# Issuing a quarter of the selected branch's cache pages from GpSimd instead of the sync engine

## The chip, the core and the metric

The kernel runs on one core of one Trainium2 chip. The metric is the device time of one execution in microseconds; the time before is the median of three runs. The profile is of one execution of its own. The engines go by the profile's names: PE is TensorE (PEld its weight loads), DVE is VectorE, ACT is ScalarE, POOL is GpSimd, SP is the sync engine, which computes nothing and issues DMA transfers. A "q" behind an engine's name (SPq) means its instruction queue: register moves, semaphores and the issuing of transfers.

## The reference

One layer of a decoder for two groups at once: a prompt of 1024 tokens and 8 sample sequences of 4 new tokens each, with 8192 tokens of past. Mixer A is a gated MLP over chunks of 128; mixer B is sparse attention with three branches (compressed blocks, selected blocks, a sliding window). What matters here is the selected branch of the sample group, cut down:

```python
past = cache_kv[page_table]            # 8 sequences x 64 pages of 128 rows, slots k_cmp, v_cmp, k_sel, v_sel
imp = sum over grouped heads of p_cmp  # importance of each block of 64 rows, from the compressed branch
sel_idx = top_k(imp with forced first, current and previous blocks, 16)
p = masked_softmax(q . k_sel[sel_idx])
o_sel = p @ v_sel[sel_idx]
o = g0 * o_cmp + g1 * o_sel + g2 * o_win
```

The pages lie in a pool in DRAM; the table says which page a sequence's n-th one is, so every page's address is known only at run time.

## The kernel before

The kernel does not gather 16 blocks. For each of the 8 sequences it loads all 64 pages of the selected keys and values (tensor `psel`, one page is 128 partitions x 1 KB = 128 KB) and puts a mask of minus infinity on the blocks that were not chosen. The work is cut into 32 groups: group n is sequence b = n // 4 and part u = n % 4, with 16 pages, four for each c in 0..3. A group goes through three steps. `sel_scores(n)` takes a page buffer, loads the pages, multiplies on PE and ends in an exponent on ACT (lines L980, L982, L983: mask added and maximum on DVE, exponent on ACT). `sel_turn` transposes the probabilities on PE (L990) and copies them out on DVE (L991); for u = 0 POOL clears a small piece (L995) that DVE then fills (L996). `sel_values` multiplies them with the values and copies the result out on ACT (L1009); that copy is the last use of the buffer.

There are four page buffers (128 partitions x 16 KB each), used in turn by `page_buffer()`: a load waits until the values of the user four places before are done. The buffers are shared with three other users: `near_scores` (the window branch, twice), `ada_late` (eight 2 MB pieces of `w_ada`, L1052) and `ya_load` at the end (L1261, L1266).

Between the groups PE works at the prompt's attention: 32 units (query tile and head) in `step`, each with `scores` (L1127, L1134 on DVE, L1129, L1135 on ACT), `turn` (PE L1160, ACT and DVE L1164), `norm` and `values`. `norm` makes reciprocal sums on DVE (L1188, L1189) and spreads them on POOL into a tile of one buffer, tag f4 (L1191); `values` of the next step transposes that tile on PE (L1200), and ends with a sum on DVE (L1211, L1212) and one on POOL (L1213). The order of PE's work in this stage is written out by hand (a manual schedule): groups are spread over the units in proportion to the units' work by the list `due`. The order on every other engine is drawn up by the scheduler from modelled times and is fixed when the program is built; each engine runs its instructions in that order.

Pages are issued by `load_pages` in fours: one register load of four table entries from SBUF (L512), then for each page a little register arithmetic and the transfer (L522). The argument `share` says which of eight fours go to ACT's queue; for the selected pages it is empty, so all 512 go to SP. `issue_after` keeps a four's register load behind the third four before it on the same queue. `mm` (L56) is the helper behind most matrix products; a "t" in a row is any tile of the kernel.

Of the kernel before, what the change touches and what calls it, by code (L numbers as in the profile page):

```python
# [50 lines left out]
def step_kernel(tc, A):  # L51
    nc = tc.nc
    sync, act, dve, pool, pe = nc.sync, nc.scalar, nc.vector, nc.gpsimd, nc.tensor

    def mm(out, lhsT, rhs, start, stop):
        return pe.matmul(out, lhsT, rhs, start=start, stop=stop)  # L56
# [30 lines left out]
    def pM():  # L87
        return psum([128, 512], F32, "M", 4)
# [407 lines left out]
        return w1s[d // 8][:, (d % 8) * 128 + 64 * s:(d % 8) * 128 + 64 * s + 64]  # L496

    b1t = C2([128, 1])
    pages, starts, freed = ([], []), [], {}

    def load_pages(items, after=None, share=(1, 4, 6), depth=2):

        for n in range(0, len(items), 4):
            i = items[n][2]
            own = len(starts) % 8 in share
            queue, kind = (act, mybir.EngineType.Activation) if own else (sync, mybir.EngineType.SP)
            before = pages[own]

            def load():
                return nc.values_load_multi_w_load_instructions(  # L512
                    ptab[i // 64:i // 64 + 1, i % 64:i % 64 + 4], engines=[kind],
                    min_val=0, max_val=639, skip_runtime_bounds_check_because="the table was clamped on chip")[1]
            with ExitStack() as order:
                if len(before) >= depth:
                    order.enter_context(tc.issue_after(before[-depth].ins))
                if own and after is not None:
                    order.enter_context(tc.issue_after(after.ins))
                rs = load()  # L520
            for (dst, src, _), r in zip(items[n:n + 4], rs):
                d = queue.dma_start(dst, src[bass.ds(r, 1)].rearrange("g p c -> p (g c)"))  # L522
            before.append(d)
            starts.append(d)
# [5 lines left out]
    def compress_load(n):  # L530
        b, half = n // 2, n % 2
        home = "b" if n >= LATE and n % 2 else "a"
        st = (R2B if home == "b" else PG)([128, 32, 256], F32, "st", 1)
        load_pages([(st[:, i], A["pcmp"], b * 64 + half * 32 + i) for i in range(32)], freed.get(home),
                   () if n == 5 else (1, 4, 6))
        paged[n] = st, home
# [119 lines left out]
    for tt in range(9):  # L656
        n = 128 if tt < 8 else 32
# [6 lines left out]
    for tt in range(9):  # L664
        n = 128 if tt < 8 else 32
# [154 lines left out]
    n = 5  # L820
# [70 lines left out]
    def page_buffer():  # L891

        n = len(uses)
        uses.append(None)
        assert n < 4 or uses[n - 4] is not None
        return n, R3S([128, 4, 4, 256], F32, f"st{n % 4}", 1), uses[n - 4] if n >= 4 else None
# [63 lines left out]
    def sel_scores(n):  # L960
        b, u = n // 4, n % 4
        if u == 0:
            sel_state[b] = (R3([128, 4], F32, "nm4", 2), R3([128, 4], F32, "s4", 2), [])
        nm4, s4, outs = sel_state[b]
        qb = QB[:, b].rearrange("p h t g -> p (h t g)")
        use, st, after = page_buffer()
        load_pages([(st[:, c, k], A["psel"], b * 64 + 16 * c + 4 * u + k) for c in range(4) for k in range(4)],
                   after, (), 3)
        s = R3([128, 544], F32, "su", 2)
        w = 512  # L970
        if u == 0:
            w = 544
            pt = pM()
            for c in range(4):
                mm(pt[32 * c:32 * c + 32, 0:32], qb, k_new[:, 0], True, True)
            dve.tensor_tensor(s[:, 512:544], pt[:, 0:32], new_sel[:, b], op=OP.add)
        ps = pM()
        for c in reversed(range(4)):
            mm(ps[32 * c:32 * c + 32], qb, st[:, c, :, 0:128], True, True)
        dve.tensor_tensor(s[:, 0:512].rearrange("p (n i) -> p n i", i=64), ps.rearrange("p (n i) -> p n i", i=64),  # L980
                          MB[:, b, 8 * u:8 * u + 8, None].to_broadcast([128, 8, 64]), op=OP.add)
        dve.tensor_reduce(nm4[:, u:u + 1], s[:, 0:w], axis=AX.X, op=OP.max, negate=True)  # L982
        act.activation(s[:, 0:w], s[:, 0:w], AF.Exp, bias=nm4[:, u:u + 1], accum_out=s4[:, u:u + 1])  # L983
        return use, st, s
# [249 lines left out]
    def sel_step(m):  # L1234

        if m:
            while m - 1 not in turned:
                one_more()
            use, st, _ = held.pop(m - 1)
            sel_values(m - 1, use, st, turned.pop(m - 1))  # L1240
            if m % 4 == 0:
                later(sel_merge(m // 4 - 1), 2)
        if m < 32:
            held[m] = sel_scores(m)

            def turning():
                turned[m] = sel_turn(m, held[m][2])
                yield from ()

            later(turning(), 3)  # L1250
# [103 lines left out]
    for gr in range(2):  # L1354
        for j in range(4):
            for h in range(2):
                own = slice(64 * h, 64 * h + 64)
# [528 lines left out]
```

## Time and profile before

| what | value |
|---|---|
| time, median of three runs (lowest to highest) | 1950.87 us (1947.74 to 1951.81) |
| profiled execution, its own time | 1950.22 us |
| its span in the trace | 1948.2 us |
| granted TensorE clock, mean | 0.982 |
| DMA packets and bytes | 253606, 345.09 MB, mean 177 GB/s |
| selected pages issued by SP | 512 of 128 KB |
| stage of the selected branch, first to last page issue | 607 to 980 us |

A row of the busy table gives an engine's busy time, its share of the span and its count of instructions. A row of the chain gives shares of the span along the work that ended last, followed back from the end. A timeline row is start, length, engine, line, operation, output<-input and count, and in square brackets the idle time before it with what ended it. A row by source line gives counts with least, median and greatest duration in nanoseconds, and the first and last start. A row of waits gives who waited for what: microseconds in total, times, and (among waits of a stretch) the longest. A row of windows gives a stretch, its length, the busy time and count of PE, PEld, DVE, ACT and POOL, the granted clock, the DMA engines' share and GB/s.

### The profile page before, as it was taken

To read this page: it belongs to the slowest core of one execution; us is meant where nothing else is said; L and a number is where in the kernel's file an instruction comes from. 1 tells how busy PE (TensorE), PEld (TensorE's weight loads), DVE (VectorE), ACT (ScalarE), POOL (GpSimd) and SP (SyncE) were. 2 spreads that over 40 slices of the span, in tenths; PEclk is the share of its full clock that TensorE was granted. 3 is DMA by queue.
4 is the path that set the end of the run, shared out by engine and by line. 5 is a ranking of instruction groups with operands and counts; after the bars stand their busy time and mean duration, and the time that the engine had idled before them with its cause. 6 is when DMAs were issued, how large, how long until landed. Compare 5 with 4: busy or idle time off the path is not lost.

```text
span 1948.2 us, 43689 instructions
## 1 busy us (share of the span) xinstructions
PE 1844.1 (95%) x16037; PEld 1734.9 (89%) x16037; DVE 1177.1 (60%) x2549; ACT 790.5 (41%) x1606; POOL 468.6 (24%) x613
## 2 busy tenths in 40 slices
PE   5899999999999998989989999899999999999996
PEld 3799999999997776767779998899999999999996
DVE  6615311112107666666665678999999999757464
ACT  4313111112116554555641356434444344545342
POOL 2410100000001000000002411567777675201010
PEclk9899999999999998999999999999999999999998
DMA  9455657776648777777764454233322223857463
GB/s 331 138 170 157 203 165 234 233 224 198 210 153 262 246 222 233 226 233 225 239 237 154 140 164 154 72 105 106 110 90 73 77 85 97 286 185 229 135 193 91
DMA packets 253606, 345.09 MB, mean 177 GB/s; under 512 B 35248, under 2 KB 189264, under 8 KB 251216
## 3 DMA queue, kind: packets, MB, share of 16 engines
q1 hardware_dynamic: 205408, 261.86, 42.8%
q10 hardware_dynamic: 36896, 41.22, 6.7%
q0 software_dynamic: 11088, 39.21, 5.7%
q8 instruction: 127, 2.08, 0.4%
q14 instruction: 87, 0.71, 0.1%
HBM read 304.91 MB, written 41.43 MB: 178 GB/s over the span
## 4 chain that ended last, share of the span: by engine, by line
PE 78%; DVE 6%; DMA 4%; issue 4%; SPq 4%; ACT 3%; POOL 1%; DVEq 0%; ACTq 0%; POOLq 0%
PE t L56 75%; SPq L522 3%; PE t L1160 2%; DMA t<-w_ada 2%; DVE t L320 1%; DMA t<-t 1%; DMA t<-psel 1%; DVE t L1591 1%; PE t L990 1%; DVE t L1529 1%; DMA t<-xT 1%; DVE t L1530 1%; DVE t L1134 0%; ACT t L1135 0%; SPq L512 0%
## 5 line engine op out<-in xcount | busy, mean ns | idle before, releaser
L56 PE MATMUL t<-t,t 128*128 128x264 f32 (+12 forms) x15262 | 1766.4, 304 | 72.1 <-DVE t L173 14.8
L56 PEld LDWEIGHTS t<-t,t 128*128 128x128 f32 (+2 forms) x15102 | 1652.2, 169 | 123.1 <-issue 50.8
L320 DVE TENSOR_TENSOR t<-t,t 128x512 fp32r<-128x512 f32 (+2 forms) x478 | 389.1, 822 | 309.4 <-ACT t L319 289.4
L319 ACT CAST t<-t 128x512 fp32r<-128x512 f32 (+5 forms) x544 | 311.1, 589 | 413.0 <-PE t L56 313.5
L1591 DVE TENSOR_TENSOR t<-t,t 128x264 f32<-128x264 f32 (+2 forms) x366 | 106.9, 338 | 11.4 <-PE t L56 11.4
L1160 PEld LDWEIGHTS t<-t,t 128*128 128x128 f32 x528 | 58.0, 144 | 31.4 <-issue 14.5
L1528 ACT ACTIVATE t<-t,t 128x1072 f32<-128x1072 f32 x44 | 56.6, 1286 | 70.1 <-DVE t L1591 44.2
L1191 POOL COPY t<-t 128x256 f32<-128x256 f32 x32 | 13.0, 407 | 281.5 <-DVE t L1189 179.2
L1164 ACT COPY t<-t 128x512 f32<-128x512 f32 (+1 forms) x112 | 58.7, 569 | 47.7 <-PE t L1160 47.6
L683 ACT ACTIVATE t<-t 128x384 f32<-128x384 f32 (+1 forms) x48 | 22.2, 465 | 137.1 <-DMA t<-pcmp 68.5
L1529 DVE SCALAR_TENSOR_TENSOR t<-t,t,t 128x1072 f32<-128x1072 f32 x44 | 72.8, 1654 | 7.7 <-ACT t L1528 7.1
L1160 PE MATMUL t<-t,t 128*128 128x128 f32 x528 | 74.5, 280 | 0.7 <-DVE t L1212 0.3
L1135 ACT ACTIVATE t<-t,t 128x640 f32<-128x640 f32 (+3 forms) x64 | 56.1, 877 | 41.3 <-DVE t L1134 36.4
L1720 POOL TENSOR_TENSOR t<-t,t 128x384 f32<-128x384 f32 (+1 forms) x12 | 13.9, 1190 | 225.9 <-ACT t L1787 225.9
L1134 DVE TENSOR_REDUCE t<-t 128x1 f32<-128x640 f32 (+3 forms) x64 | 58.8, 920 | 15.0 <-PE t L56 13.6
L685 POOL DMA_DIRECT2D t<-t x16 | 8.5, 533 | 241.6 <-DVE t L684 186.8
L1530 DVE SCALAR_TENSOR_TENSOR t<-t,t,t 128x1072 f32<-128x1072 f32 x44 | 65.1, 1479 | 0.0
L1554 POOL TENSOR_TENSOR t<-t,t 128x512 f32<-128x512 f32 x21 | 35.9, 1708 | 103.9 <-DMA t<-w_up 66.5
L1622 POOL TENSOR_TENSOR t<-t,t 128x1024 f32<-128x1024 f32 x22 | 54.3, 2468 | 16.3 <-ACT t L1621 16.3
L980 DVE TENSOR_TENSOR t<-t,t 128x512 f32<-128x512 f32 x32 | 22.1, 690 | 44.1 <-PE t L56 44.0
L1409 POOL TENSOR_TENSOR t<-t,t 128x384 f32<-128x384 f32 (+1 forms) x24 | 28.0, 1168 | 67.6 <-DVE t L1408 64.5
L320 DVE TENSOR_TENSOR t<-t 128x384 fp32r<-128x384 f32 (+1 forms) x66 | 36.1, 572 | 12.9 <-ACT t L319 12.9
(286 smaller groups left out, 1279.1 us busy)
## 6 DMA issues: line engine op xcount, KB each, us to landing
t<-psel SPq DMA_DIRECT2D x512, 128.0 KB
t<-pcmp SPq DMA_DIRECT2D x332, 128.0 KB
t<-w_down SPq DMA_DIRECT2D x120, 256.0 KB
t<-t POOLq DMA_DIRECT2D x50, 528.0 KB, 4.5
t<-w_up SPq DMA_DIRECT2D x96, 256.0 KB
t<-pcmp ACTq DMA_DIRECT2D x180, 128.0 KB
t<-w_ada SPq DMA_DIRECT2D x16, 1024.0 KB
t<-w_t ACTq DMA_DIRECT2D x52, 256.0 KB
```

What stands on the lines that cost most here:

```text
L56: return pe.matmul(out, lhsT, rhs, start=start, stop=stop)
L319: act.copy(hi, t)
L320: dve.tensor_tensor(lo, t, hi.bitcast(F32), op=OP.subtract)
L522: d = queue.dma_start(dst, src[bass.ds(r, 1)].rearrange("g p c -> p (g c)"))
L1134: dve.tensor_reduce(m4[:, branch, h:h + 1], ps[:, :, 0:w], axis=AX.XY, op=OP.max, negate=True)
L1135: act.activation(P[:, 0:L].rearrange("p (a c) -> p a c", a=2), ps[:, :, 0:w], AF.Exp, bias=m4[:, branch, h:h + 1], accum_out=s4[:, branch, ...
L1160: pe.transpose(pt[:, c:c + 128], probs[branch, h][:, 128 * b:128 * b + 128], ident)
L1164: (act.copy if w > 2 else dve.tensor_copy)(probs[branch, h][:, 128 * k:128 * (k + w)], pt[:, c:c + 128 * w])
L1528: act.activation(acc[:, 0:w], up[:, 0:w], AF.Identity, scale=cw[:, n, 0:1], bias=cw[:, n, 3:4])
L1529: dve.scalar_tensor_tensor(acc[:, 0:w], up[:, 1:1 + w], cw[:, n, 1:2], acc[:, 0:w], op0=OP.mult, op1=OP.add)
L1530: dve.scalar_tensor_tensor(acc[:, 0:w], up[:, 2:2 + w], cw[:, n, 2:3], acc[:, 0:w], op0=OP.mult, op1=OP.add)
L1591: dve.tensor_tensor(o, by4(banks[c][:, c0:c0 + n], n), other(c, c0, n) if other else o, op=OP.add)
```

## The change

Of a group's four fours the last (n = 12, which is c = 3) is issued by GpSimd; the first three stay on SP. The new value "pool" of `share` picks it, and GpSimd gets a list of its own for `issue_after`, so its register load stays behind the third four before it on GpSimd's queue. The compressed pages keep their rule. From this place on every line number is one higher in the changed kernel.

```diff
-    pages, starts, freed = ([], []), [], {}
+    pages, starts, freed = ([], [], []), [], {}
...
-            own = len(starts) % 8 in share
-            queue, kind = (act, mybir.EngineType.Activation) if own else (sync, mybir.EngineType.SP)
+            own = 2 if share == "pool" and n == 12 else int(len(starts) % 8 in share) if share != "pool" else 0
+            queue, kind = ((sync, mybir.EngineType.SP), (act, mybir.EngineType.Activation),
+                           (pool, mybir.EngineType.Pool))[own]
             before = pages[own]
...
         load_pages([(st[:, c, k], A["psel"], b * 64 + 16 * c + 4 * u + k) for c in range(4) for k in range(4)],
-                   after, (), 3)
+                   after, "pool", 3)
```

## The prediction

> **What bounds the kernel now.** I read the page first: its busy shares and the chain that ended last.
>
> ```profile
> span 1948.2 us, 43689 instructions
> PE 1844.1 (95%) x16037; PEld 1734.9 (89%) x16037; DVE 1177.1 (60%) x2549; ACT 790.5 (41%) x1606; POOL 468.6 (24%) x613
> PE 78%; DVE 6%; DMA 4%; issue 4%; SPq 4%; ACT 3%; POOL 1%; DVEq 0%; ACTq 0%; POOLq 0%
> ```
>
> TensorE bounds the whole, but 4% of the chain (some 78 us) stands on SP's queue, an engine that computes nothing. The change touches only the selected branch's pages, so the second view is the timeline of SP around them.
>
> ```profile
> 607.29 43.37 SPq L522 DMA_DIRECT2D t<-psel  x64
> ...
> 832.05 77.20 SPq L522 DMA_DIRECT2D t<-psel  x112
> ...
> 969.83 10.59 SPq L522 DMA_DIRECT2D t<-psel  x16
> 980.52 0.38 SPq L1261 DMA_DIRECT2D t<-t  x1
> 980.99 0.42 SPq L1266 DMA_DIRECT2D t<-w_ba  x1
> ```
>
> From 607.29 to 980.42 SP issues 512 pages, 16 for each of 32 groups, with no long hole: 373.1 us, or 11.66 us a group. In the long undisturbed run a page takes 77.20 / 112 = 0.69 us. Next the same stretch by kinds of instruction, count and nanoseconds (least/median/most), then a zoomed piece of the chain.
>
> ```profile
> L522 SPq FUSED_REGOPS  x512: 37/37/43, 607.1 to 980.0; - x171
> L522 SPq MOVE t<-psel x512: 29/29/38, 607.2 to 980.0; - x171
> L522 SPq DMA_DIRECT2D t<-psel x512: 332/333/1757, 607.3 to 980.1; - x171
> L512 SPq TENSOR_LOAD <-t x128: 295/301/315, 606.7 to 978.0; - x128
> ```
>
> ```profile
> 901.21 0.30 SPq L512
> 903.62 0.30 SPq L512
> ...
> 908.92 3.01 DMA t<-psel
> ...
> 912.06 1.29 PE t L56 x8
> ```
>
> One register load and four page transfers repeat every 903.62 - 901.21 = 2.41 us, 0.60 us a page: 333 + 37 + 29 ns of instructions, a quarter of the 301 ns load, and gaps of issue. The rest up to 0.69 is occasional long transfers (the 1757 ns maximum). The chain runs along these issues, through one landing of 3.01 us, into TensorE. TensorE takes groups at this pace, and between 600 and 1000 us it waited for these (microseconds in total, times, longest); below them the instruction that follows every group's scores, and what SP's queue waited for:
>
> ```profile
> PE t L990 <- ACT t L983: 12.0, 13, 2.5
> PE t L56 <- DMA t<-psel: 10.2, 4, 4.1
> ```
>
> ```profile
> L980 DVE TENSOR_TENSOR t<-t,t x32: 681/691/692, 627.5 to 985.8; 128x512 f32<-128x512 f32 x32
> ```
>
> ```profile
> SPq L522 <- DMA t<-w_ada: 19.1, 11, 3.1
> SPq L522 <- PE t L56: 4.0, 7, 1.5
> SPq L522 <- ACT t L1078: 1.2, 1, 1.2
> ```
>
> L980 follows each group's scores: (985.8 - 627.5) / 31 = 11.56 us a group, almost SP's 11.66. So the two are balanced, SP just the slower, and the price of that is 10.2 us of TensorE in four waits. That is the whole prize that the profile shows. SP itself hardly ever waits for a buffer (4.0 + 1.2 us): the buffers are free before SP gets to them. The 19.1 us behind w_ada are transfers that land late, and stay.
>
> **The change, part by part.** The sum is made against the profiled execution, 1950.22 us (1948.2 of span, 2.0 around it), 0.65 us under the median 1950.87.
>
> *Removed from SP.* For each group the last quarter goes: 1 TENSOR_LOAD and 4 pages, 2.41 us; over 32 groups 77 us at the undisturbed spacing, 128 x 0.69 = 88 us at the real one. SP keeps 12 x 0.69 = 8.3 us a group, plus its share of everything else it did in the 373.1 us (373.1 - 512 x 0.69 = 20 us, 0.6 a group): 8.9 against TensorE's 11.2 (11.56 less 10.2 / 31). SP then runs ahead until it meets the buffers' release, which is what is late next: four buffers, so about three paces or 30 us of lead where no other load sits between. I take it that the page waits go.
>
> *What the four waits are worth.* The largest is the last one, with ScalarE idle beside it:
>
> ```profile
> 984.23 1.50 PE L56 MATMUL t<-t,t 128*32 128x512 f32 x8 [4.05 <-DMA t<-psel]
> 986.87 0.59 ACT L1164 COPY t<-t 128x512 f32<-128x512 f32 x1 [6.36 <-PE t L1160]
> ```
>
> Nothing else holds TensorE there, so I count 4.05 in full. Its follow-up loads (L1261, at 980.52, waiting behind the last 16 pages on SP) come earlier too; w_ba at 980.99 does not lose. The other three make 10.2 - 4.05 = 6.15 us. Behind them stand waits for the exponent (L990 on L983, 12.0 us in 13) that could grow when TensorE is denser; I count four fifths, 4.9 us. Gain: 4.05 + 4.9 = 9 us.
>
> *Added to POOL.* Each group brings POOL one register load and four transfers with a runtime address, into its in-order stream between L1191 (the normalisers' spread), L1213 (an output sum) and L995 (a memset). POOL has never done this form; the nearest rows are its stores of the same 128 KB shape (L476), its slowest small stores (L741), and ScalarE's queue for the load.
>
> ```profile
> L476 POOL DMA_DIRECT2D o_rows<-t x18: 519/542/776, 52.6 to 113.8; - x18
> DMA to landing us min/median/max: 2.0/4.1/6.2
> ```
>
> ```profile
> L741 POOL DMA_DIRECT2D o_wsk<-t x8: 540/540/912, 589.7 to 598.9; - x8
> ```
>
> ```profile
> L512 ACTq TENSOR_LOAD <-t x45: 304/310/509, 75.9 to 558.1; - x45
> ```
>
> ```profile
> L1191 POOL COPY t<-t 128x256 f32<-128x256 f32 x32 | 13.0, 407 | 281.5 <-DVE t L1189 179.2 <-PE t L1200 39.2 <-ACT t L1202 13.8
> ```
>
> ```profile
> L1200 PE MATMUL t<-t,t x64: 272/273/422, 620.5 to 998.6; 128*128 128x128 f32 x64
> ...
> its engine sat idle before it (us, times) until:
>   POOL t L1191: 0.5, 2
> ```
>
> Low end: 4 x 0.542 + 0.310 + 4 x (0.037 + 0.029) = 2.75 us a group, 88 us in all. High end: 4 x 0.912 + 0.509 + 0.264 = 4.4 us, 141 us in all. I take the low one, since L476 has the shape. What covers it: POOL idled 281.5 us before L1191 alone, and only 2 of 32 L1200 transposes waited for L1191, 0.5 us together. Were that cover gone in every group, 32 x 2.75 = 88 us would be exposed; I charge 1 us for the two places that have no slack. A landing of 4.1 us (2.0 to 6.2) instead of SP's 3.01 costs nothing while the pages are issued a pace or more ahead.
>
> *Added wait.* POOL's first page of a group waits for the buffer, that is for the values of four groups before (L1009). Behind it in the queue stand L1191, L995 and L1213; TensorE's L1200 waits for the first, VectorE for the other two. SP had 5.2 us of such waits because it ran late; POOL has as many as the program's order gives it: bounded by 0 and, if one per group stood for a whole pace, by 32 x 11.2 = 358 us. I take 0, since the release and L1191 both follow TensorE's fixed order.
>
> *Traffic.* The bytes stay. The transfer engines have room:
>
> ```profile
> 850.00:900.00 50.00, 46.49 (x514) 34.83 (x510) 33.28 (x81) 29.87 (x68) 2.63 (x7) 0.95 0.67 198
> 604.00:1000.00 396.00, 359.14 (x4213) 275.50 (x4214) 259.03 (x696) 226.50 (x600) 29.34 (x72) 0.97 0.74 230
> ```
>
> The last three columns are granted clock, DMA share and GB/s. Pages alone move 198 GB/s at a share of 0.67, so full engines would give some 296 GB/s (an estimate from that row): 16 pages, 2.10 MB, in 7.1 us, well under 11.2. Issue is the limit, not the engines. [...]
>
> Sum: -9 + 1 = -8; 1950.2 - 8 = 1942.
>
> **The rivals.**
>
> *No change: another wait takes the place (about 1949, 1947 to 1953).* For it: 12.0 us already go to the exponent, and the clock was 0.95 in one of the stretches above; if a denser TensorE lost 0.02 of clock over 396 us, 8 us would be gone. [...] Against it: ScalarE is busy 226.50 of 396, VectorE 259.03, and the largest wait had nothing behind it.
>
> *Slower: POOL's queue holds the normalisers (about 1967).* A block of 2.75 us, or a wait for a buffer, stands ahead of L1191 in the queue, L1200 comes late, and TensorE, whose order is fixed, stops. If ten groups lose a block each: 1950.2 - 10.2 + 10 x 2.75 = 1967. It decides from 10.2 / 2.75, about four, exposed groups on. For it: the program's order on POOL is drawn up from modelled times, and the f4 tile has one buffer. Against it: the 281.5 us of idleness and 0.5 us of waits above. [...]
>
> *The pages were not the limit.* TensorE would then wait for psel as before with SP idle. The 11.56 beside 11.66 speaks against it; time 1950, inside the first rival.
>
> **How the numbers follow.** Forecast (page waits go, POOL stays covered) 0.66, its own range 1936 to 1946; no change 0.17; POOL's queue 0.17. Low end of the range: 1935, the 10.2 us plus half as much again from the 12.0 us of exponent waits moving, which I can't exclude. High end: to reach 8 in 10 it takes in the no-change case and the first exposed groups, 1950.2 - 10.2 + 5 x 2.75 = 1954. A measurement of this kernel tells 0.2%, 3.9 us, from no change; so faster 0.66, same 0.17, slower 0.17.
>
> **What would show it.** Right: SP's timeline in runs of 12 pages with waits on buffers (for TensorE or L1010 ScalarE copies) in place of unbroken issue; TensorE's waits for psel under 2 us; four POOL page transfers of about 0.54 us a group; the pace of L981 near 11.2 us; L1201 waiting for L1192 under 2 us. Wrong: POOL transfers well over 1 us, L1201 waiting for L1192 by 10 us or more, or the psel waits gone and the exponent's waits up by as much.

## The result and the profile after

The changed kernel takes 1933.87 us (median of 6, 1926.5 to 1937.59) beside 1949.93 us for the kernel before (median of 6) on the same chip: ratio 0.9919, 95% interval 0.9904 to 0.9935. It is faster, by 16 us or 0.8%, where the prediction had 8 us, and 1.1 us below the low end of its range. The profiled execution took 1933.99 us.

The order of the instructions on TensorE, VectorE and ScalarE is the same in both kernels (all 2549 rows of VectorE and 1606 of ScalarE match one by one; of TensorE's 16037, ten narrow matmuls change places with one close by); only GpSimd's and SP's differ. So the two traces can be laid side by side matmul by matmul. Line numbers after are one higher. First the page of the changed kernel: span, busy times, chain.

```profile
span 1932.4 us, 43957 instructions
PE 1842.7 (95%) x16037; PEld 1735.2 (90%) x16037; DVE 1173.3 (61%) x2549; ACT 789.2 (41%) x1606; POOL 540.8 (28%) x741
```

TensorE is as busy as before (1842.7 to 1844.1): no work went, only idle time. GpSimd gained 72 us. Next the chain of waits from 600 to 1000 us by line, before and after:

```profile
by line: PE t L56 40.7%; SPq L522 14.2%; PE t L1160 8.8%; issue 6.7%; DMA t<-psel 2.9%; PE t L990 2.7%; DVE t L1134 2.2%; ACT t L1135 2.2%; SPq L512 2.1%; DMA t<-w_ada 1.8%; ACT t L1164 1.8%; ACT t L983 1.5%; DMA t<-t 1.5%; ACT t L1129 1.2%
```

```profile
by line: PE t L56 57.7%; PE t L1161 11.7%; PE t L991 4.1%; DVE t L1135 3.1%; ACT t L1165 2.5%; ACT t L1136 2.5%; issue 2.4%; ACT t L984 2.3%; PE t L1201 1.7%; DVE t L865 1.5%; DVE t L992 1.3%; DVE t L1128 1.0%; DVE t L1165 1.0%; ACT t L1130
```

SP's page issue held 14.2% of this stretch and its register loads 2.1%; in the second line, which lists shares down to 1.0%, neither appears. Now everything of the pages (rows: count, least/median/most ns; who waited for them: us, times; landing), and SP's timeline in the second half of the stage, after:

```profile
L523 POOL DMA_DIRECT2D t<-psel x128: 546/546/628, 603.9 to 956.5; - x128
...
who waited for it (us, times):
  POOL t L523: 17.6, 8
  PEld t L56: 0.5, 2
...
DMA to landing us min/median/max: 2.6/4.1/6.7
```

```profile
821.86 0.82 SPq L1053 DMA_DIRECT2D t<-w_ada  x2
826.53 64.05 SPq L523 DMA_DIRECT2D t<-psel  x84
891.45 0.81 SPq L1053 DMA_DIRECT2D t<-w_ada  x2
897.84 17.28 SPq L523 DMA_DIRECT2D t<-psel  x24
...
954.67 7.50 SPq L523 DMA_DIRECT2D t<-psel  x12
964.56 0.38 SPq L1262 DMA_DIRECT2D t<-t  x1
```

No matmul waits for a page any more (before: 10.2 us in four waits); two weight loads do, 0.5 us together (before: two, 3.1 us). SP's queue now has holes, 821.86 + 0.82 to 826.53 for one. The waits between 600 and 1000 us say for what (us in total, times, longest), on SP, GpSimd and TensorE:

```profile
SPq L523 <- PE t L56: 62.6, 17, 6.0
...
SPq L1053 <- PE t L56: 13.9, 5, 8.2
```

```profile
POOL t L523 <- PE t L56: 25.0, 12, 6.2
...
POOL t L523 <- DMA t<-psel: 17.6, 8, 4.4
```

```profile
PE t L991 <- ACT t L984: 12.1, 14, 2.5
```

SP waits 62.6 us for buffers that TensorE still reads: it runs ahead, as forecast. GpSimd waits too, 25.0 us for buffers and 17.6 us behind its own earlier transfers, and nobody pays for it. The wait for the exponent is what it was (12.0 us in 13).

**Where the 15.7 us of the profiled spans went** (1948.15 - 1932.41). Both traces have 16037 matmuls; I cut them at the 5100th and the 9550th, which enclose the selected stage.

| stretch | before, us | after, us | difference |
|---|---|---|---|
| start to matmul 5100 | 591.34 | 591.51 | +0.2 |
| matmul 5100 to 9550 | 412.08 | 399.31 | -12.8 |
| of it TensorE idle | 38.26 | 26.41 | -11.9 |
| matmul 9550 to the last | 930.88 | 932.43 | +1.5 |
| last matmul to the last issue of o_y | 4.64 | 4.64 | 0 |
| last issue of o_y to the end | 9.21 | 4.52 | -4.7 |

The last row has nothing to do with pages at first sight. It is read from the instructions of the kernel's closing line, where each engine's queue ends with instructions that the profile calls DRAIN (of GpSimd's three the first is the long one; least/median/most in ns, first and last start in us), before and after:

```profile
L1871 POOLq EVENT_SEMAPHORE  x4: 17/17/17, 1947.4 to 1948.0; - x4
L1871 POOLq DRAIN  x3: 40/107/12252, 1935.1 to 1947.9; - x3
L1871 SPq DRAIN  x3: 7/7/7, 1942.2 to 1947.6; - x3
```

```profile
L1872 POOLq DRAIN  x3: 40/113/4255, 1924.0 to 1932.1; - x3
L1872 SPq DRAIN  x3: 7/7/7, 1931.5 to 1931.9; - x3
```

Before, GpSimd's DRAIN runs from 1935.1 for 12.25 us and ends at 1947.35; GpSimd's first semaphore instruction of that line follows at 1947.4, 5 us after SP's first DRAIN (1942.2). After, it lasts 4.26 us and ends at 1928.3, 3.2 us before SP's first (1931.5), so here SP's is the later one. In all 13 profiles below the program ends 0.8 to 0.9 us (once 1.0) after the later of the two, the end of GpSimd's long DRAIN or of SP's first.

There is a second effect inside the stage. Rows of windows on TensorE: stretch, length, busy time and count, granted clock, DMA share, GB/s, in the kernel before, right after the wait of 4.05 us at 984:

```profile
985.17:988.58 3.41, 3.41 (x16) 0.50 1.02 391
```

Half clock for 3.41 us. What it costs is seen from the same 16 matmuls on TensorE's timeline, before and after:

```profile
984.23 1.50 PE L56 MATMUL t<-t,t 128*32 128x512 f32 x8 [4.05 <-DMA t<-psel]
985.66 1.97 PE L1160 MATMUL t<-t,t 128*128 128x128 f32 x8
987.28 2.17 PE L56 MATMUL t<-t,t 128*128 128x512 f32 x8
```

```profile
974.43 1.09 PE L1161 MATMUL t<-t,t 128*128 128x128 f32 x8
975.28 1.56 PE L56 MATMUL t<-t,t 128*128 128x512 f32 x8
```

From the first start to the last end these 16 take 985.66 to 989.45, 3.79 us, against 974.43 to 976.84, 2.41 us: 1.38 us more, for the 2.92 us of half clock that fall on them (985.66 to 988.58). That is 0.47 us for each, or 1.6 us for a segment of 3.41. So in the kernel before some of TensorE's waits cost their length and this on top: of the four waits for pages, the 4.05 us had this segment behind it, the one of 2.66 us that ends at 755 shares 10.2 us of half clock with a wait for the exponent right after it, and the other two (2.23 and 1.26 us) had none.

### The profile page after: what moved, and what is told of

Its sections match the earlier page's. It is cut to its first block, busy times and chain, and to the rows that moved or that the text cites. A ratio compares the mean times of both kernels' runs of the same rounds, so it can differ in the third digit from the quotient of the medians.

```text
span 1932.4 us, 43957 instructions
## 1 busy us (share of the span) xinstructions
PE 1842.7 (95%) x16037; PEld 1735.2 (90%) x16037; DVE 1173.3 (61%) x2549; ACT 789.2 (41%) x1606; POOL 540.8 (28%) x741
## 2 busy tenths in 40 slices
DMA packets 241320, 345.10 MB, mean 179 GB/s; under 512 B 35248, under 2 KB 172880, under 8 KB 238928
## 4 chain that ended last, share of the span: by engine, by line
PE 83%; DVE 8%; ACT 4%; issue 2%; DMA 1%; POOL 1%; SPq 0%; DVEq 0%; ACTq 0%; POOLq 0%
PE t L56 79%; PE t L1161 2%; DVE t L320 1%; DMA t<-t 1%; PE t L991 1%; ACT t L319 1%; DVE t L1135 1%; DVE t L1531 1%; DVE t L1592 1%; DVE t L1530 1%; ACT t L1165 1%; ACT t L1136 1%; ACT t L984 0%; DVE t L338 0%; POOL t L1623 0%
## 5 line engine op out<-in xcount | busy, mean ns | idle before, releaser
L523 POOL DMA_DIRECT2D t<-psel x128 | 70.4, 550 | 63.8 <-PE t L56 25.0
L1165 ACT COPY t<-t 128x512 f32<-128x512 f32 (+1 forms) x112 | 58.5, 568 | 38.6 <-PE t L1161 38.4
L1136 ACT ACTIVATE t<-t,t 128x640 f32<-128x640 f32 (+3 forms) x64 | 56.1, 877 | 35.6 <-DVE t L1135 31.0
L1192 POOL COPY t<-t 128x256 f32<-128x256 f32 x32 | 13.1, 411 | 166.0 <-DVE t L1190 112.9
L711 POOL TENSOR_TENSOR t<-t,t 128x512 f32<-128x512 f32 (+1 forms) x12 | 12.3, 1041 | 125.4 <-DVE t L702 97.4
```

Source lines behind the costliest of these rows:

```text
L1136: act.activation(P[:, 0:L].rearrange("p (a c) -> p a c", a=2), ps[:, :, 0:w], AF.Exp, bias=m4[:, branch, h:h + 1], accum_out=s4[:, branch, ...
L1165: (act.copy if w > 2 else dve.tensor_copy)(probs[branch, h][:, 128 * k:128 * (k + w)], pt[:, c:c + 128 * w])
```

## The experiments

All ratios are to the kernel before, run on the same chip beside the experiment, with 95% intervals; waits for psel are those of matmuls. "Stage" is matmul 5100 to 9550, "end" the last row of the table above. The columns behind the ratio are of the profiled executions:

| kernel | ratio | waits for psel, us (times) | stage, us | half clock in it, us | GpSimd's transfers | its DRAIN, us | end, us |
|---|---|---|---|---|---|---|---|
| before | 1 | 10.2 (4) | 412.1 | 20.5 | 127 | 12.25 | 9.2 |
| quarter (the change) | 0.9919 [0.9904, 0.9935] | 0 | 399.3 | 17.1 | 255 | 4.26 | 4.5 |
| quarter again | 0.9899 [0.9878, 0.9921] | 0 | 398.0 | 13.7 | 255 | 4.25 | 4.5 |
| eighth, odd groups | 0.9888 [0.9874, 0.9902] | 0 | 396.3 | 10.2 | 191 | 8.18 | 5.1 |
| eighth, even groups | 0.9913 [0.9898, 0.9927] | 0 | 397.2 | 13.7 | 191 | 8.18 | 5.1 |
| half | 0.9932 [0.9919, 0.9945] | 0 | 405.0 | 17.1 | 383 | 6.54 | 3.6 |
| all on GpSimd | 1.0218 [1.0199, 1.0238] | 28.1 (8) | 455.8 | 58.0 | 639 | 10.14 | 7.1 |
| quarter on ScalarE's queue | 1.0062 [1.0049, 1.0075] | 0 | 418.3 | 27.3 | 127 | 12.25 | 9.2 |
| pages on SP, work on GpSimd | 0.9995 [0.9984, 1.0007] | 6.5 (3) | 411.6 | 20.5 | 127 | 12.25 | 9.2 |
| quarter, last 4 groups only | 0.9949 [0.9929, 0.9969] | 6.1 (2) | 406.3 | 20.5 | 143 | 3.76 | 3.6 |
| quarter, first 16 groups only | 0.9938 [0.9916, 0.9959] | 3.4 (2) | 404.9 | 20.5 | 191 | 8.17 | 5.3 |
| 128 small transfers on GpSimd | 0.9983 [0.9970, 0.9995] | 9.2 (3) | 411.9 | 20.5 | 255 | 4.25 | 4.1 |
| 16 small transfers on GpSimd | 0.9967 [0.9954, 0.9981] | 6.4 (3) | 406.4 | 17.1 | 143 | 3.76 | 4.3 |

The theory after the result was: SP's issue is what TensorE waited for, any relief of SP takes the waits away, and the half clock behind each wait goes with it. The rivals: GpSimd's extra work changes something by itself (the clock, the program's end); the gain needs a certain queue or a certain share; and, once the end had shown itself, that the end is a matter of the number of GpSimd's transfers or of something else.

**Half as much moved (odd groups).**

```diff
-                   after, "pool", 3)
+                   after, "pool" if u % 2 else (), 3)
```

> The last four pages go to GpSimd only in odd groups, an eighth of all pages. Theory (SP's issue pace held TensorE): SP keeps 14 pages a group, 14 x 0.69 + 0.6 = 10.3 us against TensorE's 11.2, so it is already fast enough: waits of TensorE for psel fall from 10.2 us to under 3, and TensorE's last product comes 8 to 12 us earlier than before (1934.3 in the trace of before, 1923.3 in that of the change). Rival (the gain goes with the share moved): half of it, about 5 us of psel waits left and the last product near 1929. On top of either, 4.7 us of the change's gain lie after the last product; theory: they hang on where the engines' instruction streams end and not on the pages, so they may come or not here, time 1935 or 1940; rival (they come from GpSimd being at work): about 1937.

Measured 0.9888, 1925.7 us. Sixty-four pages off SP's queue are enough: no matmul waits for a page any more. The last product came at 1913.3, 21 us earlier than before and 10 earlier than with the change, more than either side expected. That it looks faster than the quarter is mostly clock: its profiled execution had 10.2 us of half clock in the stage and 10.9 behind it, where the quarter had 17.1 and 18.7; 14.7 us less at 0.47 is 6.9 us. The repeat of the quarter below has an interval that overlaps with this one.

**Twice as much moved.**

```diff
-            own = 2 if share == "pool" and n == 12 else ...
+            own = 2 if share == "pool" and n >= 8 else ...
```

> Two fours of a group's four go to GpSimd, 8 pages, some 5.6 us a group. Theory: SP at 6 us a group and GpSimd at 5.6 plus 1 us of its own work are both far under 11.2; psel waits under 2 us, the last product within 2 us of the change's 1923.3, time within 4 us of 1934. Rival (GpSimd's in-order queue holds the normalisers): L1201 waits for L1192 by 5 us or more, time 1940 to 1960.

Measured 0.9932: no more gain than with the quarter. The waits for pages are gone there too, yet the stage is 5.7 us longer than the quarter's: 4.4 us more in which TensorE counts as busy and 1.2 us more idle, with the same 17.1 us of half clock. The scheduler also drew up another order on VectorE and ScalarE for this kernel (65 of 2549 and 43 of 1606 rows stand in another place than in the change); whether the larger share or the order makes the difference was not separated.

**The same quarter on ScalarE's queue.**

```diff
-            own = len(starts) % 8 in share
+            own = 1 if share == "act" and n == 12 else int(len(starts) % 8 in share) if share != "act" else 0
...
-                   after, (), 3)
+                   after, "act", 3)
```

> The same quarter goes to ScalarE's queue in place of GpSimd's. Theory (only SP's relief counts): psel waits under 2 us as with the change; but ScalarE issues some 2 us a group in its in-order stream, and its results are on the path, so TensorE's waits for ScalarE (L984, L1136, L1010; 12.1 + 3.7 + 0.4 us with the change) grow by 2 to 15 us; time 1936 to 1950. [...]

Slower, 1.0062, although SP is relieved just as much and no wait for a page is left; the 1959.2 us lie above the 1936 to 1950 expected. ScalarE's computing stands behind its page issues, and TensorE behind that; one wait of the stage before, then those in this kernel:

```profile
PE t L56 <- ACT t L1135: 3.7, 9, 0.7
```

```profile
PE t L991 <- ACT t L984: 16.7, 16, 3.8
PE t L56 <- ACT t L1136: 10.0, 9, 3.5
...
ACT t L1165 <- DMA t<-psel: 11.1, 8, 2.1
...
ACT t L984 <- DMA t<-psel: 7.6, 2, 4.4
```

The exponent's wait grew from 12.0 to 16.7 us and L1136's from 3.7 to 10.0; L1165 and L984 are ScalarE's own work, held up behind a page that waited for an earlier one (11.1 + 7.6 us). This is the slow rival of the prediction, on another queue, where it is real: the same pages cost or gain by what stands behind them. A part may belong to the order: some 50 rows each of VectorE and ScalarE stand in another place in this kernel than in the change, and that was not separated.

**The pages on SP, extra work on GpSimd.**

```diff
+        for _ in range(22):
+            pool.memset(R3([128, 32], F32, "pad", 1), 0.0)
```

> All pages stay on SP; GpSimd gets 22 small memsets a group, about 2.7 us, as much as the issuing takes it. Theory (GpSimd has room, SP's pace holds): psel waits stay near 10 us, L1201 waits for L1192 under 2 us, the last product within 2 us of before's 1934.3; the end after it is 9.4 us from the last output's issue as before or 4.6 as with the change, and if it is 4.6 the end hangs on GpSimd's instruction stream: time 1950 or 1945. Rival (GpSimd's time is on the path): L1201 waits for L1192 by 5 us or more, time 1955 or more.

0.9995, no difference. The waits for pages were 6.5 us and not near 10, and the last product of the profiled execution, one of the two slowest of twelve, came 4.4 us later than before's, where 2 were expected. GpSimd being busier by itself gains nothing, neither in the stage nor at the end, where the DRAIN stays at 12251 ns with 694 more GpSimd instructions in the program than before.

**The change again, beside the next three.**

> The changed kernel itself once more, beside the next three, on whatever chip they get. First measured at 0.9919 [0.9904, 0.9935] of before. If that difference belongs to the kernel: 0.990 to 0.994, TensorE waits for psel under 0.5 us in the selected stage, GpSimd's last DRAIN about 4.3 us and 4.5 us from the last issue of o_y to the end. If a part of it was that chip or that run: outside 0.990 to 0.994. For the comparison with the eighth (0.9888 [0.9874, 0.9902]): if the eighth is truly better by some 6 us, this stays at 0.992; if the two are one, this comes out near 0.989.

0.9899 [0.9878, 0.9921] at 1931.27 us, just under the 0.990 to 0.994 expected; the page waits (none), the DRAIN (4.25 us) and the end (4.5 us) are as expected. The gain belongs to the kernel; together with the two eighths (0.9888 and 0.9913) no difference between a quarter and an eighth is shown, and no version here is shown to beat the change.

**The quarter in the last four groups only.**

```diff
-                   after, "pool", 3)
+                   after, "pool" if n >= 28 else (), 3)
```

> GpSimd takes the last quarter only of the last four groups (28 to 31); the other 28 groups are as before. It isolates the last of the four waits for pages (4.05 us at 980) and what comes with it. Theory A (a wait costs itself and the half clock that follows it): the 4.05 goes and the 3.41 us at clock 0.5 behind it too, which is 4.05 + 3.41 / 2 = 5.8 us; the three earlier waits (6.1 us, half clock at 756) stay; GpSimd's last DRAIN shortens by 16 transfers' worth of (12.25 - 4.26) / 128 = 0.062 us, that is 1.0 us, to 11.2. Sum -6.8 us, ratio 0.9965. Theory B (the waits alone, by the sum of the prediction): -4.05, ratio 0.9979. Theory C (SP is late for all groups, so helping it only in the last four leaves a wait for pages near 970 to 985): under 2 us, ratio 0.999 or more.

0.9949, with Theory A's 0.9965 inside the interval (0.9929 to 0.9969). The stage shortened by 5.8 us (412.1 to 406.3), the size that the wait and its half clock make together. Its timeline has no wait near 980, and the 16 matmuls take what they take in the changed kernel:

```profile
980.77 1.09 PE L1161 MATMUL t<-t,t 128*128 128x128 f32 x8
981.62 1.56 PE L56 MATMUL t<-t,t 128*128 128x512 f32 x8
```

Yet the agreement is luck. TensorE's idle time in the stage fell by 5.7 us, and its half clock is 20.5 us as before. The earlier waits moved as well:

```profile
PE t L56 <- DMA t<-psel: 6.1, 2, 4.5
```

The one of 4.5 us ends at 807 and has 6.8 us of half clock at it, where before had a wait of 2.2 us and no half clock. The kernel with 16 small transfers below has as short a stage with all its pages on SP, so what the relief of the last four groups is worth by itself is not shown. The DRAIN missed the expectation: 3.76 us with 143 transfers, not the 11.2 that a straight line through 12.25 us at 127 and 4.26 at 255 gives.

```profile
L1872 POOLq DRAIN  x3: 40/113/3763, 1931.3 to 1938.5; - x3
```

**The quarter in the first 16 groups only.**

```diff
-                   after, "pool", 3)
+                   after, "pool" if n < 16 else (), 3)
```

> GpSimd takes the last quarter only of the first 16 groups; SP issues all pages of the groups 16 to 31. Theory A (what is gained early is kept as a lead: SP is ahead until it waits for buffers, and all 16 pages cost it 11.66 a group against TensorE's 11.2, so it loses 16 x 0.46 = 7 us of a lead of 20 to 30): no wait for psel over 0.5 us at the end either, the last wait of 4.05 gone, time like that of the eighth spread over all groups, ratio 0.989 to 0.992, DRAIN about 8.2 us with 191 transfers on GpSimd. Theory B (each group needs the relief at the time): the first waits near 752 and 758 go, the last at 980 comes back with 3 to 4 us and its half clock, ratio 0.995 to 0.996.

Between the two theories. The waits of the middle are gone and the last one is back at 2.53 us instead of 4.05: SP's lead from the first half is spent by the end.

```profile
975.84 1.29 PE L56 MATMUL t<-t,t 128*32 128x512 f32 x8 [2.53 <-DMA t<-psel]
977.06 1.78 PE L1161 MATMUL t<-t,t 128*128 128x128 f32 x8
978.49 2.59 PE L56 MATMUL t<-t,t 128*128 128x512 f32 x8
```

With the wait the slow matmuls are back, 1.78 + 2.59 us for the same 16. By this profile the relief has to last for the whole stage. The times alone do not say so: the interval of 0.9938 [0.9916, 0.9959] overlaps with that of the quarter beside it.

**Small transfers on GpSimd that nobody reads, 128 of them, pages all on SP.**

```diff
+        pad = R3([128, 4, 8], F32, "pad", 1)
+        for k in range(4):
+            pool.dma_start(pad[:, k], A["psel"][0:1].rearrange("g p c -> p (g c)")[:, 8 * k:8 * k + 8])
```

> The pages as before, all on SP; GpSimd issues beside them four transfers of 128 x 8 elements with a fixed address in each of the 32 groups (16 KB a group, read by nobody). It tells apart what the end of the program depends on: GpSimd's last DRAIN was 12.25 us with 127 transfers on GpSimd (the kernel before, and two others with 127), 8.18 with 191, 4.26 with 255, 6.54 with 383. Theory A (the number of GpSimd's transfers sets it): 255 again, so the DRAIN is about 4.3 us, 4.5 us from the last o_y issue to the end in place of 9.2, and the time is 4.7 us under before, ratio 0.9976, with the four waits for psel (10 us) still there. Theory B (it is the runtime address of the page transfers, their size, or the length of other engines' programs): DRAIN 12.25, ratio 0.9995 to 1.0005.

```profile
PE t L56 <- DMA t<-psel: 9.2, 3, 3.9
```

```profile
L1874 POOLq DRAIN  x3: 40/107/4246, 1932.5 to 1940.1; - x3
```

The waits for pages stay, and the DRAIN is 4.25 us, that of the quarter. The time is 0.9983 [0.9970, 0.9995] of before: 3.3 us (1.0 to 5.9), which fits the 5.1 us by which the end is shorter.

**The same in the last four groups only, 16 of them.**

```diff
+        if n >= 28:
+            pad = ...   # and the loop of the kernel above
```

> The pages all on SP as before; GpSimd issues four transfers of 128 x 8 elements with a fixed address in each of the last four groups only, 16 in all (read by nobody), so that it has 127 + 16 = 143 transfers, as many as the kernel in which GpSimd takes the last four groups' quarter. Theory A (the number of GpSimd's transfers alone sets its last DRAIN, by a rule that is not monotonic: 12.25 us at 127, 3.76 at 143, 8.17 at 191, 4.25 at 255, 6.54 at 383): DRAIN 3.76 us, 3.6 us from the last o_y issue to the end in place of 9.2, ratio 0.997, with the waits for psel near 10 us as before. Theory B (what those transfers are, or when they are issued, matters): DRAIN 12.25 or something new, ratio 1.000 with 12.25.

0.9967, with the DRAIN of the last-four-groups kernel to 6 ns:

```profile
L1875 POOLq DRAIN  x3: 40/107/3757, 1930.3 to 1938.1; - x3
```

These 16 were issued between 588.8 and 616.4 us, the pages of the other kernel between 934.1 and 962.8, and one has runtime addresses, the other not. Of what was varied here, only the number is common. This kernel has the waits for pages still:

```profile
PE t L56 <- DMA t<-psel: 6.4, 3, 3.1
```

Its stage is 5.7 us shorter than in the kernel before although nothing in it was to change (VectorE and ScalarE run in the order of before but for two rows each). So the waits for pages vary without anything done to the pages: 10.2, 9.2, 6.5 and 6.4 us in the four profiles with all of them on SP, in stages of 412.1, 411.9, 411.6 and 406.4 us.

**The even groups in place of the odd ones.**

```diff
-                   after, "pool", 3)
+                   after, "pool" if u % 2 == 0 else (), 3)
```

> GpSimd takes the last quarter of the even groups in place of the odd ones (an eighth of the pages, 64). Theory A (only the sum of what SP is relieved of counts, as long as it comes spread over the stage): TensorE's waits for psel at most 1.5 us, DRAIN 8.2 us with 191 transfers, stage within 3 us of the quarter's 399, ratio 0.987 to 0.992, the same as the quarter and the odd eighth. Theory B (a wait goes only where the group itself is relieved): one wait of 2 us or more left in an odd group, ratio 0.993 or more.

0.9913, no wait for a page, DRAIN 8175 ns. Odd or even groups make no difference.

**All pages on GpSimd.**

```diff
-            own = 2 if share == "pool" and n == 12 else ...
+            own = 2 if share == "pool" else ...
```

> All 16 pages of every group on GpSimd, none on SP. It looks for the point at which GpSimd's queue holds TensorE. From the rows of the quarter: 16 x (0.546 + 0.066) + 4 x 0.31 = 11.0 us of issue a group, and with the normalisers' spread (0.41 a group), the output sum and the memset 12 to 12.5, over TensorE's pace of 11.2, with waits for buffers and for its own earlier transfers on top. Theory A (issue is the limit, and now GpSimd's): TensorE waits for psel again or for L1192 by 20 us or more, 32 x 1 to 32 x 2 = 32 to 64 us more than the quarter, ratio 1.008 to 1.025. Theory B (the landing and the buffers set the pace, not the issue): ratio 0.99 to 1.00.

1.0218, 43 us slower. The waits of TensorE in the stage:

```profile
PE t L56 <- DMA t<-psel: 28.1, 8, 7.9
PE t L1201 <- POOL t L1192: 7.3, 2, 3.9
```

```profile
L523 POOL DMA_DIRECT2D t<-psel x512: 546/546/566, 603.5 to 1026.7; - x171
```

Pages late again, and now the normalisers behind them too (L1201 on L1192). The 512 page issues take (1026.7 - 603.5) / 32 = 13.2 us a group, over the pace. With the gaps came half clock: 58.0 us of it in the stage, 37.5 us more than before, some 18 us by the price above; TensorE's busy time in the stage grew by 16.1 us, its idle time by 27.5. The order on VectorE and ScalarE differs here too (127 and 124 rows). Moved whole, the issue bounds the stage again, now on GpSimd.

## What the prediction had right and which step of it failed

*SP's issue was what TensorE waited for: right.* No matmul waits for a page, SP waits for buffers (62.6 us), the stage takes 396.3 to 399.3 us in the four profiles with an eighth or a quarter moved throughout and 406.4 to 412.1 in the four with all pages on SP, and L981 runs from 627.6 to 974.5, that is 346.9 / 31 = 11.19 us a group, where 11.2 was forecast. SP's 19.1 us of waiting behind w_ada, which were to stay, fell to 3.8, with 7.6 on GpSimd.

```profile
L981 DVE TENSOR_TENSOR t<-t,t x32: 680/691/693, 627.6 to 974.5; 128x512 f32<-128x512 f32 x32
```

Issue time is what was saved, the bytes being the same (345.09 and 345.10 MB), and here it was on the path: four kernels that take an eighth to a half of the pages off SP through the whole stage, without ScalarE, came out 0.7 to 1.1% faster, of which the program's end below is some 0.2 to 0.3%.

*The three waits of the middle at four fifths: mis-sized.* They went in full, with nothing in their place. TensorE's idle time in the stage fell by 11.9 us, the 10.2 us of waits and 1.7 us of small ones; I had 9.

*One microsecond for GpSimd: it was 0.* The page transfer takes 546 ns, close to the 542 taken from L476. "I take 0" for waits of GpSimd's queue was wrong as a count (25.0 us for buffers, 17.6 us behind its own transfers) and right as a price: in the changed kernel no wait of L1201 for L1192 shows. The slow rival shows with all pages on GpSimd (7.3 us) and, in its way, on ScalarE's queue. The landing of GpSimd's pages, with VectorE busy 269.4 of 396 us, has a median of 4.1 us, that of L476 before too.

*Half clock behind a wait: left out of the sum.* The segment of 3.41 us at 985 went with its wait, some 1.6 us. But the stage has 17.1 us of half clock left of 20.5, most of it at the waits for the exponent, which both kernels have (2.54 us twice, ending at 758 and 850 here); in total TensorE's busy time in the stage fell by 0.9 us. The clock rival had it the wrong way round: a denser TensorE kept its clock (0.97 to 0.98 over 604 to 1000 us).

```profile
604.00:1000.00 396.00, 369.30 (x4298) 287.62 (x4299) 269.40 (x731) 230.59 (x608) 100.53 (x201) 0.98 0.75 240
```

*The end of the program: not in the sum at all, and the largest miss.* 4.7 us of the profiled difference. The step that failed is the list of what 128 transfers add on GpSimd: it priced their issue, and put what came with them in GpSimd's closing DRAIN (12.25 to 4.26 us) at nothing without naming it. Without these 4.7 us the time would have been 1938.6, within the range and 3 us from the forecast. The low end of 1935 had been reached by other means, the exponent's waits moving, and they did not (12.0 to 12.1 us). In the trace of before the 12.25 us DRAIN stood in the closing line's rows, and 5 us of it lay behind everything else. The two kernels with small transfers show it apart from the pages: 3.3 us (1.0 to 5.9) and 6.4 us (3.7 to 9.0; its profile had shorter page waits too), with an end that is 5.1 and 4.9 us shorter.

So the sum reads -11.9 (idle) - 0.9 (busy) - 4.7 (end) + 1.5 (given back after the stage) + 0.2 = -15.8 (-15.7 before rounding) in place of -8. What the +1.5 is was not followed up: half clock after the stage was 18.7 us against 17.3, and it swings by more than that between kernels (10.9 to 24.7), as does the whole stretch, whose work none of them changes (927.4 to 936.8 us in 13 profiles).

## What to carry to other kernels

When an engine that only issues transfers stands on the chain at a pace just over the bound's, move a thin, steady share of its issues to an engine whose queue has slack and nothing urgent behind it; here an eighth did as much as a quarter, and the whole, at 13.2 us a group, made the same bound again. Price a wait of TensorE with the half clock that may follow it (here some 1.6 us for 3.41 us of it, behind some waits and not behind others), and look at the closing line's DRAIN (here 12.25 us, 5 of them behind everything else) before the sum is made. Expect the waits themselves to vary when two paces are that close (here 11.66 and 11.56 us a group, and 6.4 to 10.2 us of waits in four profiles), and do not read a gain of their size from one profile.

## What the runs showed of the hardware

*GpSimd's closing DRAIN was equally long, to 9 ns, in profiles with equally many transfers issued by GpSimd.* 127 transfers: 12.252, 12.252 and 12.251 us (before, ScalarE's quarter, extra work). 143: 3.763 and 3.757. 191: 8.177, 8.173, 8.175. 255: 4.255, 4.253, 4.246. One profile each has 383 (6.54) and 639 (10.14). So over these six numbers it neither only rises nor only falls. The kernels with pages and with small transfers differ in the size, the time and the kind of address of what was added, and have 3.763 beside 3.757 and 4.255 beside 4.246. In all 13 profiles GpSimd had issued its last transfer 235 to 242 us before the DRAIN began. What GpSimd does in it, and whether the number is what sets its length, stays open.

*Half clock came with gaps shorter than its own length.* Its stretches in the stage lasted 3.41 us (from 848.64, 855.47 and 985.17 in the kernel before, from 832.74 in the changed one), 6.83 (from 757.65 and 849.81 in the changed one) or 10.24 (from 756.48 before). They stand at or behind gaps of 4.05 us (before, ending at 984), 2.66 and 2.54 (before, ending at 755, 761 and 855), 2.54 (the changed kernel, ending at 758 and 850) and 1.58 (the changed kernel, ending at 832); the one from 848.64 stands behind gaps of 1.35 and 0.78 us in the kernel before, while the same two in the changed one, 1.32 and 0.79, had none. Behind the gap of 2.53 in the kernel with the first 16 groups the clock was 0.62 over 976.50 to 979.90. The wait that took 1.58 us was 1.60 us in the kernel before, ending at 836, and had none behind it there, and nor had the waits of 2.23 and 1.26 us for pages. After an equal gap the length still differs: 3.41 us behind the 2.54 us that end at 855 in the kernel before, 6.83 at the same wait in the changed kernel, where it ends at 850. Two profiles of the changed kernel had 17.1 and 13.7 us of half clock in the stage, so a part of this may be the spread between executions of one kernel; no run isolates it.
